# A hybrid block of spatial gating and dilated attention: a third PSUM bank for scores and two for transposes, branch a's output split where it is made, row statistics in another pool

## The chip, the cores and the metric

The kernel runs on one core of a Trainium2 chip. The metric is device time in microseconds (us), from the start to the end of one execution. The profile is of one execution; its span is the time from the first to the last instruction.

The engines are named as in the profile: PE is TensorE's matmuls (PEld its weight loads), DVE is VectorE, ACT is ScalarE, POOL is GpSimd, SP is SyncE, which here issues nearly all DMAs, in program order (SPq in the rows).

## The reference

The input `x` has 2048 rows of 1024. One layer computes

```python
h = rmsnorm(x, g_norm)
proj = h @ w_in                     # 1024 x 9216
a_u, a_v, a_gate, q, k, v, b_gate, gate_logits = split(proj)
y_a = chunked_spatial_gating(gelu(a_u), gelu(a_v), w_s, b_s, g_v) * silu(a_gate)
y_b = dilated_attention(q, k, v) * silu(b_gate)
g_a, g_b = split(sigmoid(gate_logits))
x = x + (g_a * (y_a @ w_proj_a) + g_b * (y_b @ w_proj_b)) @ w_out
return rmsnorm(x, g_final)
```

Branch a normalises `a_v` by rows, mixes positions within chunks of 128 by a lower-triangular 128 x 128 matrix per group of 128 channels, and multiplies by `gelu(a_u)` and `silu(a_gate)`. Branch b is causal attention of 16 heads of 64 with three patterns (dilations 1, 4 and 16), each with a window of 129 keys; the three results are combined by their softmax denominators.

## The kernel before, in words

**Precision.** Every large matmul is made of three (`mm3`, L97): both operands are split into a high part, rounded to `F32R`, and the low rest, and high by high, high by low and low by high are added in PSUM. Splitting takes a cast and a subtraction: `split_X` (L141) for activations, `split_w` (L80) and `ring` (L224) for weights.

**Layout.** The 2048 tokens are four quarters (`qd`) of 512. A quarter's activations are eight tiles of 128 x 512 with channels on the partitions, each as high and low part: `X0_k_p` and `X1_k_p` (quarter modulo 2), in pool `xp`. `load_X` (L311) and `load_Y` (L837) fill the same tiles later with the outputs of the branches.

**Before the window.** `run` (L844) takes two halves of two quarters. In each, `make_h` (L155) sums the squares of the rows, brings the inverse root onto all partitions (`rsbc`, L170) and makes X; `make_T` (L183) and `make_T4` make sums and differences of X tiles, with which `unit_S` (L270) makes two quarters at once from seven products instead of eight, one step of Strassen's method. The products `prod(0)` to `prod(6)` take PSUM tiles from `bank()` (L126) in turn; VectorE drains them into `u`, `u4` and `c` and calls an evacuation function. `ev_av` (L405) sums the squares of `a_v` in `ssv`. `branch_a` (L420) has two interleaved units: `ev_u` mixes positions with a matmul into a `pt` tile (L446 to L448), `ev_g` (L455) multiplies by the gate and stores the result, 128 x 512, into `ya_d`. `T4` lies in the memory of `X1_0` to `X1_3`; at each half's end `restore` (L213) reads `xT` again (`h_chunk`, L147) and makes those four tiles anew.

**The window.** `window` (L682) interleaves attention with *fill*: the remaining projections, then branch a's output projection, one block of 128 columns at a time (`unit_T`, L320), eight matmuls at each step. A head is 12 groups of four blocks of queries, pattern 2 first. Group `j` goes through three stages: scores (`stage_s`, L551, two `ss` tiles, drained by VectorE with the bias and the row's extreme, L582, then exp on ScalarE, L588), transposes two groups later (`stage_t`, L595, one or two `pt` tiles, drained by ScalarE into `ph`, L607, and by VectorE into `pl`, L608), and outputs one group after that (`stage_o`, L613, one `po` tile, drained by ScalarE, L624). `combine` (L638) merges the three patterns of a head; after every odd head it transposes through four more `pt` tiles (L674, drained at L678). During patterns 2 and 0 `permuted` (L538) reorders keys and queries on VectorE and ScalarE (L533, L535).

**PSUM.** There are eight banks of 128 x 512 f32: two `pj`, three `pt`, two `ss`, one `po`. A tag's buffers are used in turn, so a `pt` tile has to wait until the one three before it is drained.

**The ring `ld`.** Pool `wk` has three buffers of 128 x 512 under this tag (L207, L217, L314, L494, L675, L839). `restore` takes them for `xt`, `load_X` for `xl`, `ev_pa` for the gate and `combine` for `sbg`.

**Pools.** `tp` (T tiles, `rsbc`, `ssv`), `wr` (weights) and `cp` (drained products) lie on a stack and are given up before the window; pool `wp`, which holds the window's weight blocks, starts where `tp` started, and pool `at`, with the attention's tiles, follows.

**Order.** The program records instructions in Python's order; a scheduler orders each engine's by its own estimates, and PE's order is pinned segment by segment (`seg`, L108). Every engine and SP's queue then runs in that order.

Of the kernel before, what the change touches and what calls it, by code (L numbers as in the profile page):

```python
# [9 lines left out]
F32 = mybir.dt.float32  # L10
F32R = mybir.dt.float32r
F16 = mybir.dt.float16
AF = mybir.ActivationFunctionType
ALU = mybir.AluOpType
AX = mybir.AxisListType

P = 128
D = 1024
# [9 lines left out]
class Prog:  # L28
# [8 lines left out]
    def setup(self):  # L37
        nc, tc, ctx, io = self.nc, self.tc, self.ctx, self.io
        self.const = c = ctx.enter_context(tc.tile_pool(name="const", bufs=1))
        self.ps = ctx.enter_context(tc.tile_pool(name="ps", bufs=1, space=bass.MemoryType.PSUM))  # L40
        dr = ctx.enter_context(tc.tile_pool(name="dr", bufs=1, space=bass.MemoryType.DRAM))
        self.xp = ctx.enter_context(tc.tile_pool(name="xp", bufs=1))
        self.wk = ctx.enter_context(tc.tile_pool(name="wk", bufs=2))
        self.gn = c.tile([P, KC], F32, name="gn")
        nc.scalar.dma_start(out=self.gn, in_=io["g_norm"])
        self.gv = c.tile([P, KC], F32, name="gv")
        nc.scalar.dma_start(out=self.gv, in_=io["g_v"])
        self.ident = c.tile([P, P], F32, name="ident")
        nc.scalar.dma_start(out=self.ident, in_=io["ident"])
        self.mhalf = c.tile([P, 8], F32, name="mhalf")  # L50
        nc.vector.memset(self.mhalf, -0.5)

        self.gmax = c.tile([P, 1], F32, name="gmax")
        nc.vector.tensor_reduce(out=self.gmax, in_=self.gn, axis=AX.X, op=ALU.max, apply_absolute_value=True)
        self.skq = c.tile([P, 16], F32, name="skq")
        self.sk, self.sq = self.skq[:, 0:8], self.skq[:, 8:16]
        self.sv = c.tile([P, 4], F32, name="sv")
        self.sqk = c.tile([P, 8], F32, name="sqk")
        self.niqk = c.tile([P, 8], F32, name="niqk")
        self.ihv = c.tile([P, 4], F32, name="ihv")  # L60

        self.q_d = [dr.tile([P, T], F16, name=f"q_d{h}") for h in range(NH)]
        self.k_d = [dr.tile([P, T], F16, name=f"k_d{h}") for h in range(NH)]
        self.v_d = [dr.tile([T, 130], F16, name=f"v_d{h}") for h in range(NH)]
        self.ya_d = [dr.tile([D, 512], F32, name=f"ya_d{i}") for i in range(4)]
        self.yb_d = [dr.tile([D, 512], F32, name=f"yb_d{i}") for i in range(4)]
        self.bg_d = [dr.tile([D, 512], F32, name=f"bg_d{i}") for i in range(4)]
        self.ga_d = [dr.tile([D, 512], F32, name=f"ga_d{i}") for i in range(4)]
        self.gb_d = [dr.tile([D, 512], F32, name=f"gb_d{i}") for i in range(4)]
        self.ma_d = [dr.tile([D, 512], F32, name=f"ma_d{i}") for i in range(4)]  # L70
        self.av_d = [dr.tile([T // 2, D], F32, name=f"av_d{i}") for i in range(2)]
        self.o_d = [[dr.tile([T, 66], F32, name=f"o_d{h}_{p}") for p in range(2)] for h in range(NH)]
# [48 lines left out]
        return self.ps.tile([P, 512], F32, name="pj", tag="pj", bufs=2)  # L121

    def pt(self):
        return self.ps.tile([P, 512], F32, name="pt", tag="pt", bufs=3)

    def bank(self):  # L126

        self.nbank += 1
        i = self.nbank % 7
        if i in (0, 3):  # L130
            return self.pj()
        if i in (1, 4, 6):
            return self.pt()
        return self.ps.tile([P, 2, 256], F32, name="ss", tag="ss", bufs=2).rearrange("p a b -> p (a b)")


    def alloc_X(self, tt):
# [17 lines left out]
    def make_h(self, hp, qd):  # L155
        nc, io = self.nc, self.io
        X = self.alloc_X(qd % 2)
        ss = hp.tile([P, 4], F32, name="ss", tag="ss")
        for b in range(4):
            xr = hp.tile([P, D], F32, name="xr", tag="xr", bufs=2)  # L160
            t0 = 512 * qd + P * b
            nc.sync.dma_start(out=xr, in_=io["x"][t0:t0 + P])
            nc.scalar.activation(xr, xr, AF.Square, accum_out=ss[:, b:b + 1])
        rs = hp.tile([P, 4], F32, name="rs", tag="rs")
        self.rsqrt_mean(rs, ss, 4)
        ps = self.pt()
        for i in range(4):
            nc.tensor.matmul(ps[:, i * P:(i + 1) * P], rs[:, i:i + 1].broadcast_to([P, P]), self.ident,
                             start=True, stop=True)
        bc = self.tp.tile([P, 512], F32, name="rsbc", tag=f"rsbc{qd % 2}")  # L170
        nc.scalar.copy(bc, ps)
        self.bc[qd % 2] = bc
        for k in range(KC):
            self.split_X(X, k, self.h_chunk(hp, "ht", 4, qd, k))
        return X
# [135 lines left out]
    def load_X(self, qd, src):  # L311
        X = self.alloc_X(qd % 2)
        for k in range(KC):
            t = self.wk.tile([P, 512], F32, name="xl", tag="ld", bufs=3)  # L314
            self.nc.sync.dma_start(out=t, in_=src[qd][k * P:(k + 1) * P])
            self.split_X(X, k, t)
        return X


# [84 lines left out]

    def ev_av(self, vp, hf):  # L405
        nc = self.nc
        self.ssv = self.tp.tile([P, 8, 4], F32, name="ssv", tag="ssv")

        def ev(wb, np_, ps):
            t = vp.tile([P, 2, 256], F32, name="avr", tag="avr", bufs=2)  # L410
            nc.scalar.activation(t, ps.rearrange("p (c n) -> p c n", c=2), AF.Gelu_apprx_tanh)
            j = self.cp.tile([P, 512], F32, name="junk", tag="c", bufs=1)[:, :256]
            for c in range(2):
                n = 2 * np_ + c
                nc.scalar.activation(j, t[:, c], AF.Square, accum_out=self.ssv[:, n, wb:wb + 1])
            nc.sync.dma_start(out=self.av_d[hf][256 * np_:256 * np_ + 256, wb * 256:wb * 256 + 256]
                              .rearrange("(c p) d -> p c d", c=2), in_=t)
        return ev

    def branch_a(self, ap, hf, X):  # L420
        nc, io = self.nc, self.io
        mk = ap.tile([P, P], F32, name="mk", bufs=1)
        nc.sync.dma_start(out=mk, in_=io["causal"])
        ss = ap.tile([P, 8], F32, name="ss", bufs=1)
# [30 lines left out]
        def ev_g(g, qd, ps):  # L455
            t = self.wk.tile([P, 512], F32, name="tg", tag="t5")
            nc.scalar.activation(t, ps, AF.Tanh, scale=0.5)
            nc.vector.scalar_tensor_tensor(out=t, in0=t, scalar=1.0, in1=ps, op0=ALU.add, op1=ALU.mult)
            nc.vector.scalar_tensor_tensor(out=t, in0=t, scalar=0.5, in1=um[g, qd], op0=ALU.mult, op1=ALU.mult)
            nc.sync.dma_start(out=self.ya_d[qd][g * P:(g + 1) * P], in_=t)  # L460

        qds = (2 * hf, 2 * hf + 1)
        gu = self.unit_S(X, io["w_in"], 0, ev_u, qds)
        gg = self.unit_S(X, io["w_in"], 2048, ev_g, qds)
        for g in range(2):
            gr[g] = group(g)
# [84 lines left out]
    def stage_s(self, at, G):  # L551
        nc = self.nc
        h, p, g = G["h"], G["p"], G["g"]
# [10 lines left out]
        G["S"] = S  # L564
        rng = []
        for i2 in range(2):
            ps = self.ps.tile([P, 2, 256], F32, name="ss", tag="ss", bufs=2)
            for i in range(2):
                b = 4 * g + 2 * i2 + i
                prev = b % period != 0  # L570
                n = 256 if prev else P
                q = Q[:, P * b:P * b + P] if p == 0 else Q[:, b // 4, b % 4] if p == 1 else Q[:, b]
                w = slice(P * (b + 1) - n, P * (b + 1))
                nc.tensor.matmul(ps[:, i, :n], q, KH[:, w], start=True, stop=False)  # L574
                self.pe = nc.tensor.matmul(ps[:, i, :n], q, KL[:, w], start=False, stop=True)  # L575
                rng.append(n)
            for i in range(2):
                j = 2 * i2 + i
                n = rng[j]
                bo = (0, 256, 512)[p] + (0 if n == 256 or p == 2 else P)  # L580

                nc.vector.tensor_tensor_reduce(out=S[:, j, :n], in0=ps[:, i, :n], in1=B[:, bo:bo + n],  # L582
                                               scale=self.niqk[:, pr:pr + 1], scalar=3e38, op0=ALU.add, op1=ALU.min,
                                               accum_out=ob[:, j, 65:66])
# [378 lines left out]
```

## Time and profile before

| | |
|---|---|
| three runs | 2683.05, 2691.41, 2701.62 us; median 2691.41 |
| the profiled execution | 2695.61 us, span 2693.5 us |
| mean granted PE clock | 0.975 |
| PE busy in the span | 94% |
| DMA | 411.10 MB, mean 153 GB/s |

The stages, by the first and last rows of their instructions:

| stage | us from the span's start |
|---|---|
| first half: X, v, a_v | 0 to 245 |
| first half: `unit_S` (k, q, branch a, b_gate, g_a) | 245 to 808 |
| second half: X, v, a_v | 808 to 1010 |
| second half: `unit_S` (k, q, branch a) | 1010 to 1327 |
| window: fill alone, then fill and attention | 1335 to 2300 |
| rest of branch b's projection, output projection | 2300 to 2693 |

How to read the rows: a row of a window gives its start and end, its length, and for each engine the busy time and the instructions (in brackets); then the granted clock as a share, the share of the DMA engines and the rate. A wait reads "who waited <- who ended it: us in total, times, longest". In a timeline row the numbers are start and duration, `x8` counts like rows that follow each other, and the bracket at the end is the engine's idle time before it and what ended it. PE's ends are modelled, so neighbouring matmuls overlap.

### The profile page before, as it was taken

The page shows a single profiled execution, that of the slowest core. Times are in us where ns is not written, and L with a number is a line of the kernel's source. Part 1 is how long each engine was busy: PE and PEld are TensorE (multiplying, and loading weights), DVE is VectorE, ACT ScalarE, POOL GpSimd, SP SyncE. Part 2 cuts the span into 40 slices and gives each one's busy share as a digit, 9 for nine tenths or more (in the row PEclk, how much of TensorE's full clock was granted, in tenths as well). Part 3 has the DMA queues.
Part 4 walks back from the last instruction along what each step waited for, and adds up shares of the span by engine and source line. Part 5 has one row for each costly group of instructions (what it writes and reads, how often), then busy time and mean ns, then how long its engine had stood idle before and what let it go on. Part 6 is the DMA issues. An engine that isn't in the chain of part 4 may idle for free.

```text
span 2693.5 us, 45699 instructions
## 1 busy us (share of the span) xinstructions
PE 2533.4 (94%) x17024; PEld 2154.6 (80%) x17024; DVE 1673.1 (62%) x3519; ACT 1239.6 (46%) x2455; POOL 839.9 (31%) x615
## 2 busy tenths in 40 slices
PE   5989999999998999999899999989889999899998
PEld 5989888888888998888677778878777777677787
DVE  5625757755226127567557878787989888544533
ACT  3334343343333243433357777676766665222221
POOL 0323554444444135444222222333333333100000
PEclk9989999999999999999999999999999999899999
DMA  7565343243455424433356646667676866755541
GB/s 212 115 173 155 105 122 102 98 160 126 137 172 127 102 97 125 121 99 106 91 147 163 177 133 183 175 199 210 191 218 188 235 193 193 230 175 185 166 134 64
DMA packets 473406, 411.10 MB, mean 153 GB/s; under 512 B 153184, under 2 KB 395232, under 8 KB 473184
## 3 DMA queue, kind: packets, MB, share of 16 engines
q1 hardware_dynamic: 472752, 408.11, 52.2%
q8 instruction: 134, 2.20, 0.4%
q14 instruction: 88, 0.72, 0.1%
q10 hardware_dynamic: 432, 0.07, 0.0%
HBM read 298.39 MB, written 109.71 MB: 152 GB/s over the span
## 4 chain that ended last, share of the span: by engine, by line
PE 68%; DMA 11%; DVE 11%; issue 4%; ACT 3%; POOL 1%; SPq 1%; ACTq 0%; DVEq 0%; POOLq 0%
PE pj L103 31%; PE pt L103 16%; PE ss L103 11%; PE pt L604 3%; DMA xt<-in_xT 2%; DVE S L582 2%; DMA OC<-o_d 2%; DMA v_d<-vst 2%; PE ss L574 2%; PE ss L575 1%; DMA o_d<-ob 1%; DVE pl L608 1%; PE pt L448 1%; ACT S L588 1%; SPq L392 1%
## 5 line engine op out<-in xcount | busy, mean ns | idle before, releaser
L103 PE MATMUL pj<-X,whi 128*128 128x512 f32 x1792 | 602.1, 411 | 14.4 <-POOL whi L85 8.6
L86 POOL TENSOR_TENSOR wc<-wraw,wc 128x512 fp32r<-128x512 f32 x240 | 326.1, 1364 | 366.6 <-ACT wc L83 334.8
L103 PEld LDWEIGHTS pj<-X,whi 128*128 128x128 f32 x1792 | 342.9, 195 | 86.1 <-POOL whi L85 9.0
L103 PE MATMUL pj<-X,wlo 128*128 128x512 f32 x896 | 369.6, 413 | 4.5 <-DVE wlo L86 2.6
L582 DVE CUSTOM_DVE_ANT_0 S<-ss,B,niqk 128x256 f32<-128x256 f32 (+1 forms) x768 | 284.6, 419 | 24.5 <-PE ss L575 24.2
L83 ACT CAST wc<-wraw 128x512 fp32r<-128x512 f32 x240 | 147.2, 619 | 244.3 <-PE pt L103 99.4
L608 DVE SCALAR_TENSOR_TENSOR pl<-pt,ph 128x512 f16<-128x512 f32 x320 | 204.8, 653 | 87.1 <-ACT ph L607 86.3
L103 PE MATMUL pt<-T,wc 128*128 128x512 f32 x960 | 235.7, 394 | 0.0
L588 ACT ACTIVATE S<-S,ob 128x128 f32<-128x128 f32 (+1 forms) x512 | 193.4, 437 | 73.5 <-DVE ob L582 72.5
L103 PEld LDWEIGHTS pt<-T,wc 128*128 128x128 f32 x960 | 179.7, 188 | 40.9
L85 POOL TENSOR_SCALAR whi<-wraw 128x1024 fp32r<-128x1024 f32 x64 | 71.8, 1122 | 441.4 <-PE pj L103 409.0
L103 PEld LDWEIGHTS pj<-X,wlo 128*128 128x128 f32 x896 | 175.0, 195 | 42.8 <-DVE wlo L86 5.6
L607 ACT ACTIVATE ph<-pt 128x512 f16<-128x512 f32 x320 | 177.0, 564 | 64.6 <-PE pt L604 45.3
L103 PE MATMUL pj<-WO,X 128*128 128x512 f32 x768 | 180.9, 395 | 2.6 <-ACT X L807 1.7
L103 PEld LDWEIGHTS pj<-WO,X 128*128 128x128 f32 x768 | 144.1, 188 | 38.8 <-ACT X L807 3.0
L604 PE MATMUL pt<-ident,S 128*128 128x128 f32 x1200 | 169.4, 280 | 0.4 <-DVE pl L608 0.2
L103 PE MATMUL pt<-wch,X 128*128 128x256 f32 x864 | 165.2, 289 | 4.5 <-ACT wch L83 2.3
L86 POOL TENSOR_TENSOR wlo<-wraw,whi 128x1024 fp32r<-128x1024 f32 x64 | 164.7, 2574 | 5.3
L103 PE MATMUL pj<-T,wc 128*128 128x512 f32 x672 | 165.2, 394 | 0.0
L103 PE MATMUL ss<-X,wc 128*128 128x512 f32 x672 | 162.5, 391 | 0.0
L604 PEld LDWEIGHTS pt<-ident,S 128*128 128x128 f32 x1200 | 142.9, 144 | 11.7 <-DVE pl L608 0.8
L588 ACT ACTIVATE S<-S,OC 128x256 f32<-128x256 f32 (+1 forms) x256 | 114.6, 497 | 80.0 <-DVE OC L582 79.5
(194 smaller groups left out, 5597.8 us busy)
## 6 DMA issues: line engine op xcount, KB each, us to landing
wraw<-in_w_in SPq DMA_DIRECT2D x72, 1024.0 KB, 5.7
V<-v_d SPq DMA_DIRECT2D x48, 520.0 KB, 4.3
o_d<-ob SPq DMA_DIRECT2D x32, 528.0 KB, 4.9
OC<-o_d SPq DMA_DIRECT2D x32, 528.0 KB, 5.2
xt<-in_xT SPq DMA_DIRECT2D x64, 256.0 KB, 5.0
wraw<-in_w_in SPq DMA_DIRECT2D x32, 512.0 KB, 5.0
wraw<-in_w_proj_a SPq DMA_DIRECT2D x32, 512.0 KB, 5.2
wraw<-in_w_proj_b SPq DMA_DIRECT2D x32, 512.0 KB, 4.6
```

The lines of the kernel that those rows point to most:

```text
L83: nc.scalar.copy(hi, raw)
L85: nc.gpsimd.tensor_scalar(out=hi, in0=raw, scalar1=1.0, scalar2=0.0, op0=ALU.mult, op1=ALU.add)
L86: self.w_lo.tensor_tensor(out=lo, in0=raw, in1=hi.bitcast(F32), op=ALU.subtract)
L103: self.pe = nc.tensor.matmul(out, st(a, k), mv(b, k), start=first and n == 0, stop=last and n == len(todo) - 1)
L392: nc.sync.dma_start(out=self.v_d[4 * wb + j][t0:t0 + 256].rearrange("(c p) d -> p c d", c=2), in_=t[:, :, j])
L448: nc.tensor.matmul(px[:, i * P:(i + 1) * P], av[:, 4 * q + i], w, start=True, stop=True)
L574: nc.tensor.matmul(ps[:, i, :n], q, KH[:, w], start=True, stop=False)
L582: nc.vector.tensor_tensor_reduce(out=S[:, j, :n], in0=ps[:, i, :n], in1=B[:, bo:bo + n], scale=self.niqk[:, pr:pr + 1], scalar=3e38, op0=A ...
L588: nc.scalar.activation(S[:, i, :rng[i]], S[:, i, :rng[i]], AF.Exp, bias=ob[:, i, 65:66], scale=-1.0)
L604: self.pe = nc.tensor.transpose(px[:, j * P:(j + 1) * P], G["S"][:, i, c * P:(c + 1) * P], self.ident)
L607: nc.scalar.activation(ph[:, :n], px[:, :n], AF.Copy, scale=PSCALE)
L608: nc.vector.scalar_tensor_tensor(out=pl[:, :n], in0=px[:, :n], scalar=PSCALE, in1=ph[:, :n], op0=ALU.mult, op1=ALU.subtract)
```

## The change

- `pt()` has two buffers and `ss` three. `bank()`, which hands the seven banks other than `po` to the products in turn, follows: its seventh is now an `ss` tile.
- `ya_d` has two planes. `ev_g` splits its result itself: a cast into `yah` and a subtraction into `yal`, both in the ring `ld`, each stored with its own DMA. `load_X` loads the two planes straight into the X tiles, without `xl` and without `split_X`.
- `rsbc` and `ssv` come from pool `cp` instead of `tp`.

```diff
-        self.ya_d = [dr.tile([D, 512], F32, name=f"ya_d{i}") for i in range(4)]
+        self.ya_d = [dr.tile([2, D, 512], F32, name=f"ya_d{i}") for i in range(4)]
...
     def pt(self):
-        return self.ps.tile([P, 512], F32, name="pt", tag="pt", bufs=3)
+        return self.ps.tile([P, 512], F32, name="pt", tag="pt", bufs=2)
...
-        if i in (1, 4, 6):
+        if i in (1, 4):
             return self.pt()
-        return self.ps.tile([P, 2, 256], F32, name="ss", tag="ss", bufs=2).rearrange("p a b -> p (a b)")
+        return self.ps.tile([P, 2, 256], F32, name="ss", tag="ss", bufs=3).rearrange("p a b -> p (a b)")
...
-        bc = self.tp.tile([P, 512], F32, name="rsbc", tag=f"rsbc{qd % 2}")
+        bc = self.cp.tile([P, 512], F32, name="rsbc", tag=f"rsbc{qd % 2}")
...
     def load_X(self, qd, src):
         X = self.alloc_X(qd % 2)
         for k in range(KC):
-            t = self.wk.tile([P, 512], F32, name="xl", tag="ld", bufs=3)
-            self.nc.sync.dma_start(out=t, in_=src[qd][k * P:(k + 1) * P])
-            self.split_X(X, k, t)
+            for p in range(2):
+                self.nc.sync.dma_start(out=X[k][p].bitcast(F32), in_=src[qd][p, k * P:(k + 1) * P])
         return X
...
-        self.ssv = self.tp.tile([P, 8, 4], F32, name="ssv", tag="ssv")
+        self.ssv = self.cp.tile([P, 8, 4], F32, name="ssv", tag="ssv")
...
             nc.vector.scalar_tensor_tensor(out=t, in0=t, scalar=0.5, in1=um[g, qd], op0=ALU.mult, op1=ALU.mult)
-            nc.sync.dma_start(out=self.ya_d[qd][g * P:(g + 1) * P], in_=t)
+            hi = self.wk.tile([P, 512], F32R, name="yah", tag="ld", bufs=3)
+            nc.scalar.copy(hi, t)
+            nc.sync.dma_start(out=self.ya_d[qd][0, g * P:(g + 1) * P], in_=hi.bitcast(F32))
+            lo = self.wk.tile([P, 512], F32R, name="yal", tag="ld", bufs=3)
+            nc.vector.tensor_tensor(out=lo, in0=t, in1=hi.bitcast(F32), op=ALU.subtract)
+            nc.sync.dma_start(out=self.ya_d[qd][1, g * P:(g + 1) * P], in_=lo.bitcast(F32))
...
-            ps = self.ps.tile([P, 2, 256], F32, name="ss", tag="ss", bufs=2)
+            ps = self.ps.tile([P, 2, 256], F32, name="ss", tag="ss", bufs=3)
```

PE runs the same matmuls in the same order before and after; only the names of banks differ. SP's order changes at two places. The first is the seam between branch a and the window. Before, on SP (`L460` stores branch a's results, `L150` loads `xt` for `restore`, `L91` loads weight blocks for the window, `L506` and on load the first head):

```order
L460 DMA ya_d_135<-tg 128x512
L150 DMA xt<-in_xT 128x512
L676 DMA sbg<-bg_d_140 128x512
L460 DMA ya_d_135<-tg 128x512
L676 DMA sbg<-bg_d_141 128x512
L91 DMA wraw<-in_w_in 128x8x128
L460 DMA ya_d_134<-tg 128x512
L506 DMA Q<-q_d_84 128x2048
L508 DMA KH<-k_d_100 64x2048
```

And now, with `L461` and `L464` the two stores of a result, `L485` the store of the window's first product and `L510` the load of the first head:

```order
L91 DMA wraw<-in_w_in 128x8x128 x2
L461 DMA ya_d_135<-yah 128x512
L464 DMA ya_d_135<-yal 128x512
L91 DMA wraw<-in_w_in 128x8x128
L461 DMA ya_d_135<-yah 128x512
L464 DMA ya_d_135<-yal 128x512
L91 DMA wraw<-in_w_in 128x8x128
L461 DMA ya_d_134<-yah 128x512
L464 DMA ya_d_134<-yal 128x512
L150 DMA xt<-in_xT 128x512
L485 DMA bg_d_142<-tbg 128x512
L150 DMA xt<-in_xT 128x512 x3
```

The first weight blocks moved ahead of the last stores of branch a; the `xt` loads moved behind them, and three of the four behind a store of the window. The second place is a load of branch a's output within the window (quarter 1), on SP. Before:

```order
L315 DMA xl<-ya_d_133 128x512 x2
L91 DMA wraw<-in_w_proj_a 128x8x128
L523 DMA V<-v_d_125 128x4x520
L91 DMA wraw<-in_w_proj_a 128x8x128
L489 DMA gb_d_151<-tga 128x512
L91 DMA wraw<-in_w_proj_a 128x8x128
L521 DMA V<-v_d_125 128x16x130
L489 DMA gb_d_151<-tga 128x512
L628 DMA o_d_1_177<-ob 128x1056
L315 DMA xl<-ya_d_133 128x512 x3
L635 DMA OC<-o_d_1_177 128x16x66
L315 DMA xl<-ya_d_133 128x512 x2
```

And now the end of it (nine more rows of this kind stand ahead; each first row of a tile waits for PE's last read of the old one):

```order
L315 DMA X_4_1_20396<-ya_d_133 128x512
L315 DMA X_5_0_20397<-ya_d_133 128x512
L493 DMA gb_d_151<-tga 128x512
L525 DMA V<-v_d_125 128x16x130
L632 DMA o_d_1_177<-ob 128x1056
L315 DMA X_5_1_20398<-ya_d_133 128x512
L315 DMA X_6_0_20399<-ya_d_133 128x512
L315 DMA X_6_1_20400<-ya_d_133 128x512
L315 DMA X_7_0_20401<-ya_d_133 128x512
L315 DMA X_7_1_20402<-ya_d_133 128x512
L639 DMA OC<-o_d_1_177 128x16x66
L91 DMA wraw<-in_w_proj_a 128x8x128
```

The loads moved together: sixteen of one quarter stand almost without a break, and the value tile V, the `o_d` store and the `OC` load stand between and behind them.

## The prediction

> **What bounds the kernel now.** I read the page first, then busy time by stage, then who waits in the stage that has idle time, then single rows there.
>
> ```profile
> span 2693.5 us, 45699 instructions
> ...
> PE 2533.4 (94%) x17024; PEld 2154.6 (80%) x17024; DVE 1673.1 (62%) x3519; ACT 1239.6 (46%) x2455; POOL 839.9 (31%) x615
> ```
>
> ```profile
> core 0: us, PE busy (x) PEld busy (x) DVE busy (x) ACT busy (x) POOL busy (x), PEclk, DMA share, GB/s
> ...
> 245.00:808.00 563.00, 563.00 (x2530) 463.99 (x2529) 314.46 (x411) 213.95 (x344) 269.88 (x186) 1.00 0.40 129
> ...
> 1010.00:1327.00 317.00, 317.00 (x1446) 261.38 (x1444) 212.54 (x282) 113.46 (x184) 143.61 (x104) 1.00 0.33 100
> 1327.00:1335.60 8.60, 0.04 (x1) 0.00 (x0) 5.01 (x8) 1.48 (x3) 1.05 (x1) 0.79 0.88 282
> 1335.60:1342.20 6.60, 5.34 (x12) 3.75 (x13) 0.20 (x1) 3.53 (x1) 2.35 (x1) 0.50 1.03 227
> 1342.20:1350.90 8.70, 8.70 (x39) 7.02 (x38) 6.79 (x4) 3.03 (x3) 6.19 (x3) 1.00 0.67 191
> 1350.90:2300.00 949.10, 868.49 (x8284) 729.40 (x8283) 771.04 (x2286) 643.67 (x1413) 289.83 (x204) 0.96 0.66 184
> ```
>
> The reader is to see where TensorE (PE) is not full. In the two long projection stretches, which hold branch a, it has no idle time: nothing can be gained there, and work added to VectorE (314 of 563 us) or ScalarE (214 of 563) has cover. There are two places with idle time that the change touches: the 8.6 us seam before the attention window, followed by 6.6 us at half clock, and the window itself, with 949.1 - 868.5 = 80.6 us.
>
> ```profile
> PE ss L574 <- DVE ob L582: 41.3, 60, 3.7
> PE po L623 <- DVE pl L608: 20.0, 14, 3.0
> PE po L621 <- ACT ob L624: 9.5, 9, 1.5
> ...
> PE ss L574 <- DVE OC L582: 2.5, 7, 0.6
> ...
> PE pt L604 <- DVE pl L608: 0.2, 1, 0.2
> ```
>
> These waits of PE in the window nearly make up its idle time. Half of it, 41.3 + 2.5 = 43.8 us, is a score matmul that finds both `ss` banks not yet drained by VectorE. With three `pt` banks the transposes wait 0.2 us. So the change gives a bank to the wait that exists and takes one from a wait that doesn't.
>
> **Term 1, the seam.**
>
> ```profile
> 1329.37 0.75 DVE L151 SCALAR_TENSOR_TENSOR xt<-xt,gn,rsbc 128x512 f32<-128x512 f32 x1
> ...
> 1330.18 0.38 SPq L91 DMA_DIRECT2D wraw<-in_w_in  x1
> ...
> 1334.54 1.05 POOL L85 TENSOR_SCALAR whi<-wraw 128x1024 fp32r<-128x1024 f32 x1 [29.27 <-DMA wraw<-in_w_in]
> ...
> 1335.68 2.35 POOL L86 TENSOR_TENSOR wlo<-wraw,whi 128x1024 fp32r<-128x1024 f32 x1
> ...
> 1345.39 0.61 ACT L479 ACTIVATE tbg<-pj 128x512 f32<-128x512 f32 x1 [2.75 <-PE pj L103]
> ...
> 1347.76 4.22 POOL L86 TENSOR_TENSOR wlo<-wraw,whi 128x1024 fp32r<-128x1024 f32 x1
> ...
> 1350.99 0.60 ACT L479 ACTIVATE tbg<-pj 128x512 f32<-128x512 f32 x1 [3.02 <-PE pj L103]
> ```
>
> The window's first weight block waits for the last reader of `rsbc` (1329.37), whose memory it takes over. With `rsbc` in `cp` it waits only for PE's last read of the T tiles, some three products of 2.8 us before 1327; the order on SP shows it ahead of the last stores. The first product then starts at 1327.0 instead of 1335.6 and takes 5.6 us (1350.99 - 1345.39, one product to the next), to 1332.6.
>
> But the second product needs the restored `X1`, and its four `xt` loads need slots of `ld`, which now hold `yah` and `yal` until they are stored.
>
> ```profile
> xt<-in_xT SPq DMA_DIRECT2D x64, 256.0 KB, 5.0
> ...
> ya_d<-tg SPq DMA_DIRECT2D x32, 256.0 KB, 2.0
> ```
>
> From PE's end at 1327.0: sum 0.7, tanh 0.6, two products 1.4, `yah` 0.6, `yal` 0.7, so the last store goes out at about 1331.5. The fourth weight load stands ahead of it on SP and waits until POOL has split block two (two splits of 1.05 + 2.35 to 4.22 after a landing near 1324), which may make it 1334. Then `xt` lands 3 to 5 us later, gain and cast add 1.4: PE resumes at 1336 to 1341. The fourth `xt` waits for the first one's slot (0.7), lands (3 to 5), adds 1.4; fifteen matmuls remain (3.5 us). The second product ends at 1346 to 1354, against 1350.9 before. Behind it stand Q, KH and KL, about 10 us later than before, but the first scores come only four products (22 us) on. **Term: -5 to +3; I take -1**: the wait moves from the weights to `X1`.
>
> **Term 2, the splits that leave the window.**
>
> ```profile
> L144 ACT CAST X<-xl x32: 601/618/655, 1792.7 to 2127.2; 128x512 fp32r<-128x512 f32 x32
> L145 DVE TENSOR_TENSOR X<-xl,X x32: 674/690/2890, 1794.0 to 2127.9; 128x512 fp32r<-128x512 f32 x32
> ```
>
> ```profile
> 1640.80:1694.40 53.60, 50.43 (x502) 42.62 (x500) 43.74 (x137) 39.37 (x88) 11.87 (x10) 0.97 0.57 159
> 1694.40:1752.10 57.70, 54.13 (x530) 45.93 (x527) 45.09 (x139) 39.75 (x89) 21.55 (x15) 0.97 0.66 183
> 1752.10:1811.40 59.30, 52.99 (x503) 43.44 (x502) 52.01 (x141) 42.19 (x93) 19.86 (x14) 0.94 0.67 190
> ...
> 1869.20:1926.40 57.20, 52.04 (x503) 43.43 (x501) 52.42 (x147) 42.83 (x95) 19.26 (x14) 0.94 0.72 202
> 1926.40:1985.40 59.00, 54.17 (x529) 45.91 (x526) 49.53 (x145) 38.89 (x85) 21.11 (x15) 0.97 0.72 209
> 1985.40:2046.80 61.40, 52.57 (x503) 43.42 (x501) 56.30 (x149) 41.44 (x90) 19.15 (x14) 0.94 0.79 218
> ...
> 2106.00:2164.40 58.40, 51.86 (x503) 43.57 (x501) 51.37 (x149) 41.41 (x90) 20.71 (x14) 0.94 0.82 232
> ```
>
> Each row is one head. Heads 7, 9, 11 and 13 hold the four loads of branch a: 59.3 + 57.2 + 61.4 + 58.4 = 236.3 us. Head 5 has the same matmuls (502) and none: 53.6. Four of those are 214.4, so 21.9 us are in question. Even heads grow as well with no load (57.7 to 59.0), from other work on VectorE; for all four heads I take off 9 us for that. **Term: -9 to -22; I take -13.**
>
> Part of this comes through the clock: those heads show 0.94, head 5 and the even heads 0.97.
>
> ```profile
> 1426.00:1437.80 11.80, 9.86 (x106) 8.31 (x106) 10.62 (x30) 9.65 (x17) 0.80 (x1) 1.00 0.60 150
> 1437.80:1444.60 6.80, 5.74 (x24) 4.28 (x20) 6.80 (x23) 3.78 (x9) 1.52 (x2) 0.50 0.07 24
> ```
>
> In the first stretch PE idles 1.9 us in all, and the clock is then at half for 6.8 us: a short wait costs more than itself. [...]
>
> The same 32 casts and 32 subtractions are added in branch a: 32 x 0.62 = 20 us of ScalarE, 32 x 0.69 = 22 us of VectorE, under PE's gapless stretches. Uncovered they would cost 42; with 214 and 314 of 563 us busy I take 0. Four tanh-gate results per pass take two `ld` slots each, a store lands in 2.0 us, and three slots turn over faster than one result per 2.8 us product. The mixing tile's `pt` bank was drained a product earlier: 0.
>
> **Term 3, the banks.** I paired each of the 384 score tiles in the window with the drain of the tile three before it: all had ended at least 0.59 us earlier. So at fixed times all 43.8 us vanish. I paired the 352 `pt` tiles (320 of L604, 32 of L674) with the drain (L608 or L678) of the tile two before: 76 start too early, by 47 us together, the first at 1503.1, the last at 2303.1. One of them:
>
> ```profile
> 1645.13 2.42 DVE L644 TENSOR_TENSOR mn<-mn,OC 128x16 f32<-128x16 f32 x1
> ...
> 1647.76 0.68 DVE L608 SCALAR_TENSOR_TENSOR pl<-pt,ph 128x512 f16<-128x512 f32 x1
> ```
>
> ```profile
> 1647.08 1.03 PE L604 MATMUL pt<-ident,S 128*128 128x128 f32 x8
> ```
>
> Its second four transposes (1647.5) write the third bank now; with two they need the bank that L608 drains until 1648.4. PE's order does not change, and scores stand directly ahead of transposes: a score that no longer waits for VectorE hands its wait to the transposes, whose drain is later in VectorE's order. Behind a waiting transpose stand the fill matmuls and the output matmuls, and behind those ScalarE's `ob` copy. Bounds -44 and +47. The four heads of term 2 hold 17 of the 44 and 15 of the 47, and go with the splits; of the rest, 27 against 32, **I take +5**.
>
> [...]
>
> **Term 4, twice the bytes.** The 32 loads of branch a become 64, 8.4 MB more to write and to read. At 232 GB/s for a DMA share of 0.82 the engines move 283; a load of 4.2 instead of 2.1 MB takes 7.4 us longer, four times. Its rows also wait on SP, for PE's last read of each X tile, with V, OC, weight and store transfers queued behind. Weights are two blocks ahead. 0 to 30; I take +3.
>
> **The sum.** -1 - 13 + 5 + 3 = -6. The profiled execution took 2695.6 us (span 2693.5 and 2.1 around it), 4 above the median of 2691.4; I carry -6 to the median: **2685 us**, own range 2668 to 2702.
>
> **The rivals.** (1) VectorE's lateness comes in short bursts that the third score bank bridges, and the transposes find their drains done. For it: with three score banks the slack is nowhere under 0.59. Against it: 76 early starts. With all 43.8: -1 - 13 - 44 + 3 = -55, 2636; with half, 2658. (2) **Slower:** the transposes' 47 us come in full, and the 44 don't go, because VectorE (771 of 949 us) sets the pace in the same bursts: -1 - 13 + 47 + 3 = +36, 2727. It decides once PE's wait before L604 and L674 has grown by over 11 us more than the score wait fell. For it: scores and transposes are adjacent. Against it: four heads lose their splits. (3) It does not do what it says: `X1` as late as the weights were, the splits' heads stay long as even heads do: 0 + 0 + 5 + 3, 2699.
>
> **How the numbers follow.** Forecast 0.50, rival 1 0.25, rival 2 0.13, rival 3 0.12. A measurement here tells about 1% (27 us) from no change. Faster by more than that: nearly all of rival 1 and little of the forecast, 0.24. Slower: most of rival 2, 0.10. The rest, 0.66, lies within 1%. The range 2650 to 2714 holds the forecast, half of rival 1 and part of rival 2.
>
> **What would show it.** Right: PE gapless to about 1332 and then idle some 5 us before `X1` at L103; no X casts on ScalarE between 1790 and 2130; heads 7, 9, 11, 13 shorter by 2 to 5 us each; the score wait under 10 us and the wait before L604 and L674 at 20 to 50. Wrong: transposes waiting under 10 us (rival 1), score waits still over 30 (rival 2), PE waiting for V, or idle time in branch a.

## The result and the profile after

The changed kernel takes 2731.98 us (median of 4 runs, 2728.14 to 2742.85), the kernel before 2689.68 us beside it (4 runs, 2683.05 to 2701.62). The ratio is 1.0161, 95% interval 1.0136 to 1.0186: **slower by 42 us**, where 2685 was forecast. The result lies above the range, on the side of the second rival (2727).

The first view is the page of the changed kernel: its span, and each engine's busy time.

```profile
span 2731.5 us, 45787 instructions
...
PE 2543.3 (93%) x17024; PEld 2150.0 (79%) x17024; DVE 1694.2 (62%) x3519; ACT 1245.7 (46%) x2455; POOL 840.5 (31%) x615
```

The second is its busy time by stage: the two long projection stretches, the end of the seam, and the time from the first score's drain on VectorE to the last.

```profile
core 0: us, PE busy (x) PEld busy (x) DVE busy (x) ACT busy (x) POOL busy (x), PEclk, DMA share, GB/s
245.00:808.00 563.00, 562.14 (x2504) 459.65 (x2503) 341.39 (x426) 219.18 (x356) 267.85 (x183) 1.00 0.42 137
1010.00:1327.00 317.00, 316.58 (x1439) 259.93 (x1437) 229.47 (x290) 118.37 (x194) 144.37 (x106) 1.00 0.36 113
1340.00:1350.90 10.90, 9.27 (x23) 5.65 (x24) 5.57 (x8) 2.48 (x4) 0.00 (x0) 0.62 0.71 193
...
1374.60:2313.30 938.70, 834.05 (x8029) 695.23 (x8029) 723.77 (x2223) 624.57 (x1364) 273.06 (x191) 0.95 0.66 188
```

For the last row, the same two drains in the kernel before:

```profile
1374.50:2278.80 904.30, 829.68 (x8030) 697.86 (x8029) 753.75 (x2255) 635.14 (x1396) 272.18 (x190) 0.96 0.66 186
```

Branch a is as full as it was, though VectorE has 27 us more in its first stretch (341 against 314) and 17 in its second (229 against 213): that work did have cover. The first score stands where it stood. All but a few of the lost microseconds lie between first and last score: 938.7 against 904.3, with the same matmuls. PE's idle time there grew from 74.6 to 104.7 us, its busy time by 4.4, at a granted clock of 0.95 instead of 0.96. VectorE is busy 30 us *less*. The waits of PE from 1352 to 2340 us, which takes in that stretch, name what ended the idle time:

```profile
PE pt L608 <- DVE pl L612: 24.9, 37, 2.7
PE po L627 <- DVE pl L612: 19.8, 15, 3.1
PE pj L103 <- POOL whi L85: 17.5, 2, 9.0
PE ss L578 <- DVE ob L586: 13.6, 22, 2.5
PE po L625 <- ACT ob L628: 12.3, 14, 1.5
PE pt L678 <- DVE pl L612: 10.9, 9, 3.1
```

(From here on lines of the window stand 4 further down in the changed kernel: L578 is L574 of before, L608 is L604, L612 is L608, L678 is L674.) The score wait fell from 43.8 to 13.6 us, as it was meant to. The transposes' wait, 0.2 before, is now 24.9 + 10.9 and some 3 in smaller rows. And there is a wait that the kernel before did not have: 17.5 us in two pieces, for the split weights of the projection, in heads 11 and 13. SP's and POOL's rows show the first piece:

```profile
1994.75 2.38 POOL L86 TENSOR_TENSOR wlo<-wraw,whi 128x1024 fp32r<-128x1024 f32 x1
...
2005.80 2.35 POOL L86 TENSOR_TENSOR wlo<-wraw,whi 128x1024 fp32r<-128x1024 f32 x1
...
2042.88 1.05 POOL L85 TENSOR_SCALAR whi<-wraw 128x1024 fp32r<-128x1024 f32 x1 [6.85 <-DMA wraw<-in_w_proj_a]
```

```profile
2017.49 0.38 SPq L527 DMA_DIRECT2D V<-v_d  x1
2017.91 1.45 SPq L315 DMA_DIRECT2D X<-ya_d  x3
2022.46 0.32 SPq L502 DMA_DIRECT2D ma_d<-ma  x1
2022.83 6.97 SPq L315 DMA_DIRECT2D X<-ya_d  x13
...
2034.01 0.32 SPq L632 DMA_DIRECT2D o_d<-ob  x1
2034.43 0.38 SPq L525 DMA_DIRECT2D V<-v_d  x1
2037.55 0.34 SPq L502 DMA_DIRECT2D ma_d<-ma  x1
2037.98 0.39 SPq L91 DMA_DIRECT2D wraw<-in_w_proj_a  x1
```

```profile
2043.98 1.22 PE L103 MATMUL pj<-X,whi 128*128 128x512 f32 x2 [8.96 <-POOL whi L85]
```

Raw weight blocks (`wraw`) have two buffers, used in turn. The one that the next block takes is free when POOL's subtraction ends at 1997.13; the subtraction that starts at 2005.80 is the other buffer's. The block is requested only at 2037.98, 40.9 us after its buffer came free: on SP it stands behind all 16 transfers of the `X` load, and behind stores and V loads that wait for the attention in their turn. The 16 transfers hold SP for 8.4 us (1.45 + 6.97); most of the rest is such waiting. The block's split starts at 2042.88, and PE, with 8.96 us of waiting, goes on only at 2043.98. In the kernel before, SP has three weight blocks among the eight `xl` loads of head 11, and the first is requested 19.1 us after its buffer came free (1981.19):

```profile
1978.79 2.40 POOL L86 TENSOR_TENSOR wlo<-wraw,whi 128x1024 fp32r<-128x1024 f32 x1
...
2000.31 0.38 SPq L91 DMA_DIRECT2D wraw<-in_w_proj_a  x1
```

So the theory to test was: two separate losses, the transposes' bank and the order of the loads on SP, and a seam that stays as it was because another ring now holds it.

### The profile page after: what moved, and what is told of

Its sections match the earlier page's. It is cut to its first block, busy times and chain, and to the rows that moved or that the text cites. A ratio compares the mean times of both kernels' runs of the same rounds, so it can differ in the third digit from the quotient of the medians.

```text
span 2731.5 us, 45787 instructions
## 1 busy us (share of the span) xinstructions
PE 2543.3 (93%) x17024; PEld 2150.0 (79%) x17024; DVE 1694.2 (62%) x3519; ACT 1245.7 (46%) x2455; POOL 840.5 (31%) x615
## 2 busy tenths in 40 slices
DMA packets 482623, 427.89 MB, mean 157 GB/s; under 512 B 154208, under 2 KB 396256, under 8 KB 482400
## 4 chain that ended last, share of the span: by engine, by line
PE 66%; DVE 14%; DMA 11%; ACT 4%; issue 4%; POOL 1%; SPq 1%; DVEq 0%; ACTq 0%; POOLq 0%
PE pj L103 30%; PE ss L103 17%; PE pt L103 11%; PE pt L608 3%; DVE S L586 3%; DVE pl L612 2%; DMA OC<-o_d 2%; DMA xt<-in_xT 2%; DVE OC L666 1%; DMA wraw<-in_w_out 1%; DMA wraw<-in_w_in 1%; PE ss L578 1%; ACT S L592 1%; PE ss L579 1%; DMA o_d<-ob 1%
## 5 line engine op out<-in xcount | busy, mean ns | idle before, releaser
L103 PE MATMUL pj<-X,whi 128*128 128x512 f32 x1792 | 604.5, 412 | 29.8 <-POOL whi L85 17.5
L103 PEld LDWEIGHTS pj<-X,whi 128*128 128x128 f32 x1792 | 343.1, 195 | 103.9 <-POOL whi L85 18.0
L103 PE MATMUL pj<-X,wlo 128*128 128x512 f32 x896 | 369.8, 413 | 7.8 <-POOL wlo L86 5.3
L612 DVE SCALAR_TENSOR_TENSOR pl<-pt,ph 128x512 f16<-128x512 f32 x320 | 204.8, 652 | 147.6 <-ACT ph L611 143.1
L103 PE MATMUL ss<-X,wc 128*128 128x512 f32 x960 | 233.4, 395 | 0.0
L103 PEld LDWEIGHTS ss<-X,wc 128*128 128x128 f32 x960 | 179.7, 188 | 42.4
L103 PEld LDWEIGHTS pj<-X,wlo 128*128 128x128 f32 x896 | 174.8, 195 | 46.5 <-POOL wlo L86 7.8
L608 PE MATMUL pt<-ident,S 128*128 128x128 f32 x1200 | 176.0, 280 | 28.0 <-DVE pl L612 24.9
L103 PE MATMUL pt<-T,wc 128*128 128x512 f32 x768 | 186.6, 392 | 0.9 <-DVE tm L449 0.9
L103 PE MATMUL pj<-WO,X 128*128 128x512 f32 x768 | 182.2, 398 | 4.4 <-ACT X L811 4.3
L608 PEld LDWEIGHTS pt<-ident,S 128*128 128x128 f32 x1200 | 140.6, 144 | 50.4 <-DVE pl L612 34.9
L103 PEld LDWEIGHTS pj<-WO,X 128*128 128x128 f32 x768 | 145.3, 190 | 40.7 <-ACT X L811 5.6
L103 PEld LDWEIGHTS pt<-T,wc 128*128 128x128 f32 x768 | 143.9, 188 | 32.4 <-ACT wc L83 1.0
L103 PE MATMUL pj<-T,wc 128*128 128x512 f32 x672 | 163.9, 392 | 0.0
L103 PE MATMUL ss<-wch,X 128*128 128x256 f32 x832 | 155.1, 285 | 5.9 <-ACT wch L83 5.9
```

Of the source, the lines that this page charges most:

```text
L103: self.pe = nc.tensor.matmul(out, st(a, k), mv(b, k), start=first and n == 0, stop=last and n == len(todo) - 1)
L608: self.pe = nc.tensor.transpose(px[:, j * P:(j + 1) * P], G["S"][:, i, c * P:(c + 1) * P], self.ident)
L612: nc.vector.scalar_tensor_tensor(out=pl[:, :n], in0=px[:, :n], scalar=PSCALE, in1=ph[:, :n], op0=ALU.mult, op1=ALU.subtract)
```

## The experiments

### Each part alone

The kernel before with one part of the change; and the change with its banks put back. Differences to the kernel before are its time, 2690 us, times the ratio less one, and differences between runs are those of their ratios.

The banks alone (`pt` 3 to 2, `ss` 2 to 3, the rotation `bank()` as in the change):

> The kernel before with the banks alone: three for scores, two for transposes. Theory A (the loss has two parts, the banks and the order of the loads on SP): the wait before scores falls from 44 us to 10-20, the wait before transposes grows from 0 to 30-45, and the time is 12 to 28 us above the kernel before. Rival B (the trade of banks is even, and the whole loss comes with the splits and their loads): within 6 us of the kernel before. Rival C (the prediction's second rival, the banks carry the whole loss): 35 to 47 us above it.

Measured: 2724.02 us, ratio 1.0133 (1.0110 to 1.0157), 36 us slower: more than theory A gave, and at the lower end of rival C. PE's waits between first and last score:

```profile
PE pt L604 <- DVE pl L608: 31.2, 45, 2.7
PE po L623 <- DVE pl L608: 21.6, 15, 3.0
PE ss L574 <- DVE ob L582: 20.4, 25, 3.7
PE po L621 <- ACT ob L624: 15.8, 15, 3.3
PE pt L674 <- DVE pl L608: 8.7, 9, 3.1
```

The transposes' wait is 40 us, the score wait still 20, and PE's wait before the output matmuls 37.4, which is 8 more than before. The score wait lost 23 us and the other two took 48.

The splits alone (`ya_d` in two planes, `yah` and `yal`, loads straight into `X`):

> The kernel before with branch a's output split where it is made and loaded as two planes, banks and pools as before. Theory A: the four heads with the loads lose VectorE and ScalarE work, but all transfers of a load stand together in SP's order with the weights behind them, so that PE waits 15 to 20 us for branch a's projection weights in heads 11 and 13; net +5 to +18 us. Rival B (the whole loss is here): +30 to +45. Rival C (the prediction's term 2: the work leaves the window and the loads cost little): -5 to -15.

Measured: 2711.78 us, ratio 1.0091 (1.0071 to 1.0112), 24 us slower, more than theory A gave. The wait for the weights is there (16.6 us). What theory A had left out is at the seam:

```profile
1343.19 1.22 PE L103 MATMUL pj<-X,whi 128*128 128x512 f32 x2 [20.20 <-POOL whi L85]
```

With `rsbc` in the old pool the weight block waits for its last reader, that for the `xt` loads, and those for ring slots of `ld` that `yah` and `yal` hold: 20.2 us instead of 8.6.

The pools alone (`rsbc` and `ssv` in `cp`):

> The kernel before with the row statistics' broadcast and the sums of V in the constant pool alone. Prediction's term 1 carried over (the reload of the input rows is held by its buffer ring, not by this tile): within 4 us of the kernel before, PE's wait at the seam of branch a and the window moves to another tile and the first score stays within 2 us of 1374. Rival: in this kernel nothing else holds the ring, the reload starts under branch a, and the first score comes 5 to 9 us earlier.

Measured: 2684.22 us, ratio 0.9981 (0.9968 to 0.9995), and the first score at 1368.0 (1374.0 in the kernel before). That is the rival: without branch a's split outputs the move is worth about 5 us.

The changed kernel with `pt` 3 and `ss` 2:

> The changed kernel with the banks of before put back (two for scores, three for transposes). Theory A: the score wait is back at 35-45 us, the transposes' wait gone, the wait for the weights in heads 11 and 13 stays at 15-20; 5 to 18 us above the kernel before. Rival B (no loss from the banks): 36 to 46 above it, as the changed kernel. Rival C (the banks carry it all): 5 to 15 below it.

Measured: 2705.57 us, ratio 1.0065 (1.0046 to 1.0085), 17 us slower than before and 26 faster than the change: theory A. The score wait came back to 33 us only, not to 35 to 45.

### What the banks do

One bank taken away and none given (`pt` 2, `ss` 2):

```diff
-        return self.ps.tile([P, 512], F32, name="pt", tag="pt", bufs=3)
+        return self.ps.tile([P, 512], F32, name="pt", tag="pt", bufs=2)
...
-        i = self.nbank % 7
+        i = self.nbank % 6
```

> The kernel before with two banks for scores, two for transposes and one bank unused. Theory A (the third transpose bank is worth more than the third score bank, and both are worth something): the score wait of the kernel before, 35-45 us, stands beside a transpose wait of 35-50; 45 to 65 us above the kernel before, and so 10 to 30 above the run with the banks alone (+36). Rival (VectorE's pace sets what both wait for, and a third score bank only moves the wait): as the run with the banks alone, +30 to +42.

Measured: 2724.98 us, ratio 1.0132 (1.0116 to 1.0149), the same as with the third score bank: the rival holds. With two score banks PE waits 40.2 us before scores, with three 20.4, and no difference in time can be told:

```profile
PE ss L574 <- DVE ob L582: 40.2, 53, 3.7
PE pt L604 <- DVE pl L608: 22.4, 29, 5.0
PE po L623 <- DVE pl L608: 19.7, 14, 3.1
PE po L621 <- ACT ob L624: 9.6, 11, 1.4
PE pt L674 <- DVE pl L608: 8.0, 9, 3.0
```

Of the 20 us that the third score bank saves before scores, 18 stand, in its rows above, as 9 more before L604, 6 before L621, 2 before L623 and 1 before L674. From first to last score its profiled execution is 5.5 us shorter (934.0 against 939.5), so a small gain is not excluded.

The merge's transposes (L674) in the scores' three banks, with the banks alone:

```diff
-            px = self.pt()
+            px = self.ps.tile([P, 2, 256], F32, name="ss", tag="ss", bufs=3).rearrange("p a b -> p (a b)")
             for r in range(4):
```

> The run with the banks alone (three for scores, two for transposes), with the 32 transposed tiles of the heads' merge (L674) taken from the scores' three banks instead. Theory A (the merge's tiles are what the two banks lack, since even heads grew most): the transposes' wait falls from 46 us to 10-25, the score wait stays under 30, and the time is 10 to 25 us below the run with the banks alone (+36). Rival (the 320 tiles of the attention's own transposes need the third bank): within 6 us of that run.

Measured: 2710.40 us, ratio 1.0068 (1.0049 to 1.0088), 17 us below the banks alone: time as in theory A. Its account holds only in part. The 8.7 us before L674 are gone, but L604 still waits 32.8, not 10 to 25. From first to last score the run is 16.3 us shorter, 7.4 of it idle time; the other 8.9 are busy time of the same matmuls, at a granted clock of 0.97 instead of 0.96.

Does a third score bank pay while the transposes keep three? Two kernels with one bank for the fill's products (one of the two early products of the last stage then takes a `pt` bank), with two and with three score banks:

```diff
-        return self.ps.tile([P, 512], F32, name="pj", tag="pj", bufs=2)
+        return self.ps.tile([P, 512], F32, name="pj", tag="pj", bufs=1)
```

> The kernel before with one bank instead of two for the fill's products (one bank unused), two for scores, three for transposes. It is the base for the next run: score wait 35-45 us, transposes' wait under 3, and a product of the fill waits for the one before it to be drained; 10 to 60 us above the kernel before.

> The same with a third score bank. Theory A (VectorE's order hands the wait on, whatever the transposes have): within 8 us of the run with one product bank, with the waits before outputs and transposes up by most of what the score wait loses. Theory B (a third score bank pays once the transposes keep their three): the score wait falls by 20 to 40 us, the transposes wait under 10, and the time is 15 to 40 us below that run.

Measured: 2730.05 us (1.0148, 1.0130 to 1.0166) with two, 2725.02 us (1.0142, 1.0121 to 1.0164) with three. Time and idle say theory A: no difference that can be told. First to last score, two score banks, then three:

```profile
1376.30:2297.60 921.30, 835.45 (x8031) 698.49 (x8029) 753.92 (x2253) 636.22 (x1396) 271.43 (x190) 0.96 0.65 182
```

```profile
1380.40:2295.70 915.30, 826.65 (x8030) 693.78 (x8029) 751.77 (x2253) 635.64 (x1396) 272.14 (x190) 0.96 0.65 183
```

PE idles 85.9 us with two and 88.7 with three, though the score wait falls from 37.6 to 20.7 us. It went to the products (PE's waits for `ma`, `tga` and `tbg` in this stretch: 28.1, then 38.3), which theory A had not named, and by some 5 us each to the outputs and to the transposes. Here too the stretch itself is a little shorter with three, by 6.0 us.

The five banks of scores and transposes in one ring, taken in the order in which tiles are allocated:

```diff
-        return self.ps.tile([P, 512], F32, name="pt", tag="pt", bufs=3)
+        return self.ps.tile([P, 512], F32, name="pt", tag="st", bufs=5)
...
-            ps = self.ps.tile([P, 2, 256], F32, name="ss", tag="ss", bufs=2)
+            ps = self.ps.tile([P, 2, 256], F32, name="ss", tag="st", bufs=5)
```

> The kernel before with the five banks of scores and transposes in one ring, taken in the order of allocation. Theory A (the waits come from how the five banks are divided, each kind being short at other moments): scores' and transposes' waits together under 30 us (44 before) and the time 8 to 30 us below the kernel before. Rival B (VectorE's drains come late in its own order whatever the banks): within 6 us of the kernel before. Rival C (a score tile now waits for transposes' drains, which come last): 15 to 50 above it.

Measured: 2672.55 us, ratio 0.9931 (0.9917 to 0.9945), 19 us faster than before: theory A.

```profile
1368.20:2257.00 888.80, 818.16 (x8030) 687.40 (x8029) 755.12 (x2255) 634.76 (x1396) 266.89 (x190) 0.97 0.67 189
```

The same 8030 matmuls take 818.2 instead of 829.7 us, and the idle time is 70.6 instead of 74.6: of the 15.5 us by which this stretch is shorter, 11.5 are busy time of the same matmuls, at a granted clock of 0.97 instead of 0.96.

### What the loads do

The transfers of a load given out two at a time, behind each of eight weight blocks (change, banks of before):

```diff
             W = self.wblock(self.wp, w, c0 + nb * P, P)
+            if rows is not None:
+                rows(nb)
```

> The changed kernel with the banks of before, and the 16 transfers of a load of branch a given out two at a time behind each of eight weight blocks. Theory A (the loss of the splits is the weights queued behind the 16 transfers on SP): PE's wait for the weights in heads 11 and 13 falls from 17 us to under 3, head 8 loses its extra 3, and the time is 17 to 28 us below the run with the banks put back (+15), so 2 to 13 below the kernel before. Rival (it is the doubled bytes): the wait stays over 10 us or moves to X, and the time within 6 us of that run.

Measured: 2680.44 us, ratio 0.9967 (0.9955 to 0.9979), 26 us below the run with the banks put back: theory A. No wait for POOL's weights is left, and the heads with the loads, 7, 9, 11 and 13, are these (the rows of the changed kernel first):

```profile
1760.60:1818.80 58.20, 51.99 (x502) 43.12 (x500) 46.21 (x138) 40.48 (x89) 19.98 (x13) 0.94 0.73 217
1882.50:1941.70 59.20, 52.25 (x503) 43.40 (x500) 47.05 (x140) 40.39 (x87) 21.88 (x15) 0.94 0.81 241
2002.20:2070.90 68.70, 53.93 (x502) 44.01 (x500) 45.28 (x143) 39.45 (x84) 19.55 (x15) 0.88 0.79 232
2131.20:2197.20 66.00, 53.23 (x503) 43.63 (x500) 44.18 (x143) 38.81 (x84) 19.81 (x15) 0.90 0.82 237
```

```profile
1750.50:1807.60 57.10, 52.05 (x502) 43.32 (x501) 45.39 (x137) 39.95 (x89) 19.95 (x15) 0.94 0.73 208
1865.30:1921.30 56.00, 50.90 (x502) 42.70 (x501) 46.73 (x140) 39.53 (x87) 20.04 (x15) 0.94 0.86 254
1979.70:2035.10 55.40, 51.68 (x507) 43.18 (x506) 49.55 (x143) 38.11 (x84) 20.18 (x15) 0.97 0.87 257
2093.40:2148.30 54.90, 51.38 (x506) 42.97 (x505) 47.20 (x143) 38.44 (x84) 20.89 (x15) 0.97 0.89 259
```

The four sum to 223.4 us, against 236.3 in the kernel before and 252.1 in the changed one. The bytes are the same as in the changed kernel (427.89 MB), moved at up to 259 GB/s: the bytes as such show no cost in these rows.

The changed kernel whole, with nothing but that edit:

> The changed kernel whole, with nothing but the transfers of branch a's loads given out two at a time. Theory A (the order on SP and the banks are separate losses): PE's 17 us of waiting for weights in heads 11 and 13 vanish and the time falls by 18 to 30 us, to 2700-2713, still 10 to 23 above the kernel before, which is the banks' part less the splits' gain. Rival (VectorE behind in its drains uses those pauses to catch up): the transposes' wait grows by what the weights' wait falls, and the time is within 8 us of the changed kernel.

Measured: 2713.77 us, ratio 1.0077 (1.0058 to 1.0097), 23 us below the change: theory A. The order of the loads costs about as much beside the one set of banks as beside the other.

The seam: the last input rows reloaded through the five buffers of `um`, before branch a's pool closes (change, banks of before):

```diff
-            self.split_X(X[1], k, self.h_chunk(self.wk, "ld", 3, qd, k))
+            self.split_X(X[1], k, self.h_chunk(pool, tag, bufs, qd, k))
...
                     drain(branch_a)
+                    if hf == 1:
+                        self.restore(X, qds[1], self.wq, "um", 5)
```

> The changed kernel with the banks of before, and the four last input rows before the window reloaded through branch a's five buffers of mixed values instead of the ring that now holds branch a's split outputs. Theory A (that ring held the reload): the first score at 1366-1369 instead of 1373.6, 5 to 8 us below the run with the banks put back. Rival (the reload is not what the seam waits for): the first score stays within 2 us of 1373.6, time within 3 of that run.

Measured: 2691.47 us, ratio 1.0007 (0.9995 to 1.0018), 16 us below the run with the banks put back, more than theory A gave. The first score came at 1361.8. The time to the first score differs by some microseconds from one execution to the next: VectorE drains that score at 1362.4 here and at 1368.7 in the run with both edits, which differs from this one only in the window's loads. From the last start of a long stretch (the stall near 862) to the first score it took 511.1 us with the banks put back and 499.7 here, so the ring held 11 us; the other 5 of the 16 are not accounted for. PE's stall for `X`, in the changed kernel and in this one:

```profile
1341.47 1.52 PE L103 MATMUL pj<-X,whi 128*128 128x512 f32 x2 [7.56 <-ACT X L144]
```

```profile
1335.25 0.49 PE L103 MATMUL pj<-X,whi 128*128 128x512 f32 x1 [1.41 <-ACT X L144]
```

### Together

Both edits, with the banks of before:

> Banks of before; pools and splits of the change; transfers given out two at a time, and the last input rows reloaded through the ring of mixed values. Theory A (the seam and the order on SP are separate losses): the two gains add, first score 11 to 12 us earlier than with the transfers alone given out, 2664 to 2672 us. Rival (an earlier seam only meets a later wait): within 3 us of that run, 2677 to 2683.

Measured: 2669.53 us, ratio 0.9919 (0.9898 to 0.9941): theory A.

And with the ring of five:

> The run before this one with the five banks of scores and transposes in one ring. Theory A (the ring takes away the waits of every head, the splits those of four): a further 10 to 20 us, 2646 to 2660. Rival (both take the same waits, of the heads that held the splits): within 6 us of the run without the ring.

Measured: 2647.07 us, ratio 0.9828 (0.9807 to 0.9849), 46 us faster than the kernel before: theory A again, with a gain of 24 us over the run without the ring where 10 to 20 were expected.

```profile
1358.70:2232.00 873.30, 813.96 (x8030) 685.69 (x8029) 731.79 (x2223) 619.57 (x1364) 267.66 (x191) 0.98 0.71 204
```

First to last score it is 31 us shorter than before: 15.3 less idle, 15.7 less for the same matmuls.

## Why the prediction was wrong, point by point

**Term 1, the seam (-1): right, and for the reason given.** The weights are waited for 1.9 us instead of 9.8 (8.6 and 1.2); PE waits 7.56 us for the restored `X1` (5 forecast), resumes at 1341.5, at the late end of the forecast (1336 to 1341), and the first score is unmoved. That the `ld` ring holds the reload is shown: another ring freed 11 us. The working had the last store of branch a at about 1331.5, or 1334 behind a weight load; it went out at 1335.4. It took 0.7 us for each of VectorE's operations there, and in the stretch in which POOL splits the first two weight blocks (1324.7 to 1332.7) two of them take 2.7 and 2.9 us.

**Term 2, the splits that leave (-13): right in size, not in what the change does with it.** With the loads given out two at a time the four heads are 12.9 us shorter than before. Head 5 was a favourable base: head 3 has no load either, took 55.7 us at a clock of 0.94, and four of those leave 13.5 us in question instead of 21.9. In the changed kernel the four heads are 15.8 us longer, mostly because the same edit brought the wait of term 4. The cover assumed in branch a held, though VectorE is 44 us busier there, twice the 22 forecast.

**Term 4, twice the bytes and SP's queue (+3 of 0 to 30): the mechanism was named, the size was wrong.** The step that failed is "Weights are two blocks ahead". PE waited 8.96 us for a request at 2037.98, so one by 2029.0 would have done: the cover was 32 us from the buffer's release, and the request came after 40.9. The term measured 26 us beside the banks of before and 23 beside those of the change. What lay in reach before the run was the order of SP's transfers: in head 11 three weight blocks among eight loads before, none among the 16 after. The 7.4 us per load for bytes did not show.

**Term 3, the banks (+5 of -44 to +47): the sign was right, the size was wrong.** The banks alone measured +36. Beside the splits, where the forecast stood, they measured +26 (the change against the change with its banks put back), and +30 with the loads given out two at a time. The step that failed is "So at fixed times all 43.8 us vanish", set as a gain beside the 47. With fixed times a drain that PE no longer waits for seems free; in the runs the score wait fell by 20 and 17 us with a third bank, and other waits of PE grew by about as much. What that bank is worth was measured twice, with two transpose banks and with three: the times show no difference, to within some 5 us, and nothing near 44. The best reading is that the next tile, in whichever bank, waits for the same VectorE. It is not proved, for the scheduler also changed VectorE's order between the two kernels of each pair, in some 50 places among 3519 instructions, and what that does was not separated. The pairing gave the other side better: 47 us forecast, of which 40 came as waits before transposes. So the two ends were not of one kind, and "of the rest, 27 against 32" weighed them as if they were.

**The sum.** From the kernel before, the splits and pools with the loads given out two at a time bring -9, the order of the loads +26, the banks +26: +43 (by the ratio) in all. These are steps of one chain, so they must add up; the other way round the banks bring +30 and the order +23. The two parts measured apart, +36 for the banks and +17 for the rest, sum to 53, 10 more than the whole. The prediction had expected part of the banks' price to go with the splits; the intervals, 5 to 7 us to each side of each, do not settle it.

**The rivals.** The second rival came nearest, in mechanism and in time, but in its time by luck as well: it has 47 us for the banks, which beside the splits measured 26, and the difference was made up from a place that it did not name, the wait for the weights (23 to 26 us). Its account of the 44 us held in part: the score wait did fall, by 30 us, but the kernel's time did not. Its point of decision was met with the banks alone (transposes' wait up 40, score wait down 23), but not in the changed kernel itself, where 39 stood against 30: the waits before outputs and the clock had to be counted too. Of the signs of a wrong forecast that were listed, none is this one; a wait for POOL at L103 was missing from the list. The range failed because SP's term was taken at a tenth of its bound, and because -44 was given weight as an end.

What stays open: how the score wait passes to outputs, products and transposes was read from sums, not followed drain by drain; why the ring of five leaves the idle time nearly as it was and yet shows a higher clock; and whether the transfers on another queue would do as well as giving them out two at a time was not tried.

## What to carry to other kernels

A wait that ends with an engine's drain need not be gained when another bank takes it away: give the bank and see whether the time and PE's *idle* time fall, not whether that row of the waits falls (here, with two transpose banks, the score wait fell from 40.2 to 20.4 us, and no difference in time could be told). A bank taken from a neighbour whose wait is zero can cost much of what the pairing of tile and drain says (here 36 us of 47). A load that becomes more transfers, even with less work behind it, must be placed in the queue's order: look at what stands behind it, and spread it among what is due first (here that was worth 23 to 26 us).

## What the runs showed of the hardware that was not expected

The granted clock goes with much of what the ring of five, and every edit together, gain between first and last score. In the kernel before and in the ring of five, the same 8030 matmuls are busy for 829.7 and 818.2 us, and the idle time hardly differs (74.6 and 70.6); with every edit together they take 814.0. By the clock's own records in these traces, PE runs at half clock for 68 us between first and last score before, for 48 with the ring of five and for 41 with every edit. Half of what is saved of that, 10 and 14 us, is nearly the saving in busy time (11.5 and 15.7). The waits are short ones: with the ring of five, where the clock is 0.97 instead of 0.96, the list shows 3.2 us at most for scores, outputs and the attention's transposes.

Half clock stands beside short waits elsewhere too. In the kernel before, head 11 had one wait of PE of 3.7 us and head 13 none over 2.6 us, and both show a clock of 0.94. With the loads given out two at a time (and the change's pools and splits) PE idles 3.7 and 3.5 us in these heads instead of 8.8 and 6.5, and both show 0.97. This fits the prediction's reading that a short wait costs more than itself; which wait brings the half clock, and from what length on, no run tested.
